# Scores' low-part product on 128 rows, and the maps' last product in 64x64 array tiles: a two-layer hybrid backbone on one Trainium2 core

## Chip, core and metric

The kernel runs on one core of a Trainium2 chip, in one launch. The metric is the device time in microseconds (us) from the first to the last instruction of an execution, with what lies around it; lower is better. TensorE multiplies (PE in the rows; PEld is its weight load), VectorE (DVE), ScalarE (ACT) and GpSimd (POOL) do the rest, and SyncE (SP) issues all DMAs in one queue, in order. Each engine works through its own instructions in the order in which they stand.

## What is computed

Two layers over 512 latent and 256 context tokens of width 1024. A layer is a gated feed-forward half, a token mixer, and a second feed-forward half. The mixer projects the tokens once and gives the columns to three groups of heads: a Fourier transform, a banded attention with six query heads on two key heads, and a recurrence in both directions. The change touches the last two. Cut to what matters here:

```python
# attention: per block of 128 queries, keys of up to three blocks and all 256 context keys
s_w = jnp.einsum('bnqhgd,bnkhd->bnhgqk', qb, kw)
s_c = jnp.einsum('bnqhgd,bchd->bnhgqc', qb, kc)
m = max(s_w.max(-1), s_c.max(-1), sink)
o = (exp(s_w - m) @ vw + exp(s_c - m) @ vc) / den

# recurrence, per head, over time, in both directions; the latent scan starts from the context's state
sa = state @ a
state = state * w + sa[..., None] * b + v[..., None] * k
y = state @ r
```

## The kernel before

**Precision.** Products that need more than one pass are made of exact splits: a float32 value is cut into a high part (float32r) and a low part, and high x high, low x high and high x low are summed in PSUM. A float32r matmul is one record in the trace. The recurrence uses plain float32 matmuls, and each of these is two records in the trace.

**Attention** (`attention`). Work goes by blocks of 128 queries: blocks 4 and 5 are context, 0 to 3 latent; the first layer does all six, the second the four latent ones. `queries(b)` loads the queries of a block for both key heads (384 KB, `q<-qd`, L1062) into the tile `t`, of which there is one buffer. ACT casts `t` to high parts in `qs` (L1064, one buffer, too), and POOL writes the low parts `t - qs` over the half of the partitions that belongs to the other key head (two instructions, L1067). So for key head v the 64 partitions of its own half hold high parts, and the other 64 hold low parts. `scores` then makes each score tile with two float32r matmuls: all 128 rows of `qs` against the keys' high parts, which lie on both halves (L1083: high x high and low x high in one), and the 64 high rows against the keys' low parts `kl` (L1084). A block has six heads; a latent head has two such pairs (256 context keys, and 256 or 384 window keys), a context head has one. That is 108 pairs: 84 of 256 columns and 24 of 384.

**Recurrence** (`rwkv`). Time is cut into chunks of 64 tokens and groups of four chunks; six groups per layer. For each group `stage_a` forms products of the operands (PSUM tiles `pa`), `inverses` inverts triangles on DVE, `stage_c` builds every chunk's map of state and values (PSUM tiles `pb`), and `chain` carries the state through the four chunks (`pz`). The last product of `stage_c` (L1350) multiplies, for each of three head pairs and four chunks, a 64-row half of AA (stationary, 128 columns) with BL (128 columns wide, or 64 in the two context groups of the second layer), one PSUM tile `ps[h]` per half. DVE adds the tiles to the maps MG (L1352), and the chain reads those. All matmuls of the recurrence go through the helper `mm`, so they have line L1261 in the trace; the last product is `pb<-HB` with stationary `64*128`.

**What sets the order.** The code is emitted group by group; every microsecond of estimated recurrence work `mm` calls `pump`, which emits steps of attention, of the next modulations (`wmod`, L251 to L272) and of the attention heads' part of the output projection (`out_part`, L1532). A scheduler then simulates the engines and places each instruction on its engine in the order of the simulated times, so a change of a wait or of an instruction's size moves others.

**Names.** `kf[0]`, `kf[1]`: the keys' high parts (`k` in rows); `kf[2]`: low parts (`kl`). `AA` and `BL` lie in the tile `HB`. `at`: PSUM tiles of attention (two). `wq`, `hh`, `pq`: other parts of the layer.

Of the kernel before, what the change touches and what calls it, by code (L numbers as in the profile page):

```python
# [32 lines left out]
# tiles of the feed-forward columns in the chunks after the first; buffers of gated products: raw (then low), high  # L33
# [5 lines left out]
class Halves:  # L39
    """Products of weights and tokens by Strassen's scheme (Winograd's form): the halves are of the  # L40
    inner dimension, of the tokens, and gates with values; 7 products of quarters instead of 8."""

    def __init__(self, net, n0, n):
        self.net, self.nc, self.w = net, net.nc, n // 2
        hi, lo = net.hT["h"], net.hT["o"]
        m = self.w
        q = lambda x, t, k: x[:, 4 * k:4 * k + 4, n0 + t * m:n0 + t * m + m]
        self.a = {f"a{t + 1}{k + 1}": (q(hi, t, k), q(lo, t, k)) for t in range(2) for k in range(2)}
        # the quarter a21 isn't needed by itself
        self.a["s3"] = self.a["a21"]  # L50

    def sums(self, anchor):
        """The second half of the work comes behind the anchor."""
# [31 lines left out]
    def weights(self, wi, c0):  # L85
        """The quarters of a tile of gates and one of values, and their sums."""
# [13 lines left out]
    def unit(self, ws, sg, pool):  # L100
        """silu(gates) * values."""
# [42 lines left out]
# buffers of the ring of weights that stay through the mixers' projections, and more: raw, split  # L144
# [3 lines left out]
class Net:  # L148
# [78 lines left out]
    def behind(self, inst, anchor=None):  # L227
        """The engine of both issues inst after the anchor."""
# [10 lines left out]
    def mod_steps(self, l, m, wp, pf):  # L239
        """Steps for the modulation m of layer l: the sums by quarters of the array, then their sums with the bias."""  # L240
# [35 lines left out]
    def mod(self, l, ms, stg, rows):  # L276
        """The modulations ms (at most two) of layer l."""
# [34 lines left out]
    def norm_cols(self, l, n, m_shift, m_scale):  # L312
        """Columns of g*(1+scale) and of shift, by stream."""
# [8 lines left out]
    def gate_row(self, l, n, m, s, half):  # L322
        """The row half*m*g, on all partitions."""
# [11 lines left out]
    # The arena's tiles hold rows in turn (4), loaded rows (2), halves of transposes (2) and gate rows (2);  # L335
    # in the feed-forward halves the sums of quarters of the normed tokens
# [18 lines left out]
    # In the passage from one part to the next the engines keep to the order of the program  # L355
# [10 lines left out]
    def squares(self, x, junk):  # L366
        """The root of the mean of the squares."""
# [18 lines left out]
    def prenorm(self, t, x, cols, xn, junk):  # L386
        """Normalises the token tile t; every second one is transposed with the one before it. Two steps."""
# [11 lines left out]
    def flush(self, rest=True):  # L399
        """Emits the transposes that were put off, behind products that needn't wait for them."""  # L400
# [8 lines left out]
    def some(self, n=1):  # L409
        """What follows the transposes, by quarters."""  # L410
        for _ in range(min(n, len(self.bits))):
            self.bits.pop(0)()
# [37 lines left out]
    def residual(self, t, o, grow, xn, po):  # L450
        """x + norm(o)*grow for the token tile t, with o's halves as they come. Three steps."""
# [3 lines left out]
        for i in range(2):  # L455
            cs = slice(i * 512, i * 512 + 512)
            # of the halves' mean squares
# [11 lines left out]
    def passage(self, toks, outs, post):  # L469
        """The last products of the tokens, by halves (outs), and what follows them, a token behind."""  # L470
# [27 lines left out]
    def load_w(self, srcs, shape):  # L498
        """Loads weights (pieces by columns, or by rows of two dimensions)."""
# [11 lines left out]
    def turning(self, j, name, shape, dt):  # L511
        """The next tile of the ring, raw (0) or split (1)."""
# [9 lines left out]
    def cut(self, x, e=None):  # L522
        """Splits x, of at most 512 columns in all, exactly: (high, low), each of float32r."""
# [9 lines left out]
    def split_w(self, srcs, shape, e=(None, None)):  # L533
        """Weights, split exactly, by halves of their first free dimension."""
# [4 lines left out]
    def prod(self, ps, w, s, c0, n):  # L539
        """Sums in ps the products of the weights w with n tokens of stream s, from c0."""  # L540
# [13 lines left out]
    def ffn(self, l, wi, wo, toks, post, last, mods=(), early=None):  # L554
        """last: loads that follow the last chunk's products with the tokens."""
# [10 lines left out]
        # the last 64 columns come first: gates and values in one tile  # L566
# [12 lines left out]
        def split_g(sg, w):  # L579
            gh = fp.tile([128, NT], F32R, name="gh", bufs=GB)  # L580
            if w == 64:
                # the low parts below the high ones
# [10 lines left out]
        def gated(sg, cs, w, pg, pu):  # L593
            """silu(gates) * values; of a tile with both, on its upper half."""
# [9 lines left out]
        def first(ch):  # L604
            """The first chunk, by pairs of token tiles, as they become ready."""
# [81 lines left out]
    def early_keys(self, l, raw):  # L687
        """The context's keys of the recurrence, while the latent tokens are on their way."""
# [10 lines left out]
    def mixer(self, l, need_ctx):  # L699
# [5 lines left out]
        with self.pool("mixo", bufs=1) as mo, ExitStack() as outer:  # L705
# [8 lines left out]
            # partial output projections: of the Fourier heads, and of the attention heads as well  # L714
            self.part = [[self.dp.tile([128, D], F32, name=f"part{l}_{j}_{i}") for i in range(6)] for j in range(2)]
            # decays over the chunks
            pcs = mo.tile([128, 2, 3, 12], F32, name="pcs")
            self.rw = dict(pcs=pcs)
            # in DRAM: head sums times values; values in token-major; queries; by direction the recurrence's
            # unit keys by the decay so far, rates and keys by its inverse, receptances by the decay  # L720
# [6 lines left out]
            # keys' high parts, on both halves, by head; low parts  # L727
# [1048 lines left out]
```

## Time and profile before

| | us |
|---|---|
| median of 3 runs | 3582.73 |
| lowest and highest run | 3574.76, 3584.79 |
| span of the profiled execution, first to last instruction | 3573.4 |
| PE busy in that span | 3262.0 (91%) |
| stretch of the recurrence and attention, first layer | 886 to 1336 |
| the same, second layer | 2756 to 3140 |

The profiled execution's own time is not listed apart from its span; the lowest of the three runs lies 1.4 us above that span and the median 9.3 us. In rows of the timeline the first number is the start in us, the second the length of a run of equal instructions with the modelled end of the last; the difference of two starts is therefore the better price. `128*128 128x256` is the stationary operand's rows and columns, then the moving operand's rows and columns.

### The profile page before, as it was taken

The page shows a single profiled execution, that of the slowest core. Times are in us where ns is not written, and L with a number is a line of the kernel's source. Part 1 is how long each engine was busy: PE and PEld are TensorE (multiplying, and loading weights), DVE is VectorE, ACT ScalarE, POOL GpSimd, SP SyncE. Part 2 cuts the span into 40 slices and gives each one's busy share as a digit, 9 for nine tenths or more (in the row PEclk, how much of TensorE's full clock was granted, in tenths as well). Part 3 has the DMA queues.
Part 4 walks back from the last instruction along what each step waited for, and adds up shares of the span by engine and source line. Part 5 has one row for each costly group of instructions (what it writes and reads, how often), then busy time and mean ns, then how long its engine had stood idle before and what let it go on. Part 6 is the DMA issues. An engine that isn't in the chain of part 4 may idle for free. (4 is left out here: it accounts for less than half of the span.)

```text
span 3573.4 us, 51830 instructions
## 1 busy us (share of the span) xinstructions
PE 3262.0 (91%) x19801; PEld 2729.5 (76%) x19801; DVE 2352.3 (66%) x4374; ACT 1378.0 (39%) x2818; POOL 809.4 (23%) x609
## 2 busy tenths in 40 slices
PE   7999998998778897999998999998995898979998
PEld 5689997776556655899997899997774676758997
DVE  4577777456466656677777767777464666467897
ACT  3333335342334334433335433335342433344444
POOL 0222222023101013322222322222041000024333
PEclk9999999999889988999999999999997878779999
DMA  5432224245667556222224222224355563253333
GB/s 179 148 119 71 71 69 138 87 141 134 153 172 177 160 187 214 60 69 68 71 71 140 61 71 65 71 71 138 97 166 119 157 157 71 68 182 89 101 107 101
DMA packets 540346, 410.13 MB, mean 115 GB/s; under 512 B 210405, under 2 KB 462188, under 8 KB 540098
## 3 DMA queue, kind: packets, MB, share of 16 engines
q1 hardware_dynamic: 540098, 406.82, 39.4%
q8 instruction: 156, 2.56, 0.3%
q14 instruction: 92, 0.75, 0.1%
HBM read 345.60 MB, written 61.16 MB: 114 GB/s over the span
## 5 line engine op out<-in xcount | busy, mean ns | idle before, releaser
L666 PE MATMUL po<-wq,gh 128*128 128x512 f32 (+1 forms) x1936 | 692.4, 408 | 43.6 <-ACT po L458 23.8
L529 ACT CAST wq<-raw 128x512 fp32r<-128x512 f32 (+1 forms) x626 | 383.7, 619 | 619.0 <-PE pq L112 438.8
L112 PE MATMUL pq<-hh,wq 128*128 128x384 f32 (+1 forms) x2432 | 612.8, 324 | 5.1 <-DVE st L132 2.1
L530 DVE TENSOR_TENSOR wq<-raw,wq 128x512 fp32r<-128x512 f32 x616 | 510.5, 838 | 102.3 <-ACT wq L529 97.0
L112 PE MATMUL pq<-arena,wq 128*128 128x384 f32 (+1 forms) x2736 | 491.5, 324 | 1.7 <-ACT st L116 1.1
L666 PEld LDWEIGHTS po<-wq,gh 128*128 128x128 f32 (+1 forms) x1936 | 368.6, 191 | 152.6 <-ACT po L458 31.0
L112 PEld LDWEIGHTS pq<-arena,wq 128*128 128x128 f32 x2736 | 451.3, 189 | 24.1 <-issue 4.3
L112 PEld LDWEIGHTS pq<-hh,wq 128*128 128x128 f32 x2432 | 431.6, 188 | 19.5 <-issue 5.7
L112 PE MATMUL pq<-ho,wq 128*128 128x384 f32 (+1 forms) x1216 | 394.1, 324 | 0.0
L666 PE MATMUL po<-wq,go 128*128 128x512 f32 x924 | 371.0, 402 | 2.6 <-DVE go L590 2.6
L529 ACT CAST wq<-t 128x512 fp32r<-128x512 f32 x228 | 140.7, 621 | 340.6 <-PE pq L112 303.2
L93 POOL TENSOR_TENSOR t<-raw 128x512 f32<-128x512 f32 x76 | 103.6, 1363 | 735.8 <-DVE wq L530 358.6
L672 DVE TENSOR_TENSOR accl<-accl,po 128x512 f32<-128x512 f32 x288 | 196.8, 684 | 100.8 <-PE po L666 99.0
L112 PEld LDWEIGHTS pq<-ho,wq 128*128 128x128 f32 x1216 | 229.3, 189 | 7.1 <-issue 0.9
L544 PE MATMUL pil<-hh,wq 128*128 128x512 f32 (+1 forms) x704 | 217.0, 387 | 7.9 <-DVE hh L432 5.6
L666 PEld LDWEIGHTS po<-wq,go 128*128 128x128 f32 x924 | 177.1, 192 | 32.5 <-DVE go L590 5.7
L530 DVE TENSOR_TENSOR wq<-t,wq 128x512 fp32r<-128x512 f32 x228 | 176.4, 779 | 28.3 <-ACT wq L529 23.5
L544 PE MATMUL pc<-hh,wq 128*128 128x256 f32 x976 | 179.1, 284 | 6.4 <-DVE hh L432 5.1
L97 POOL TENSOR_TENSOR t<-raw,t 128x512 f32<-128x512 f32 x76 | 117.1, 1540 | 283.2 <-DVE wq L530 283.1
L987 DVE TENSOR_TENSOR W<-W 96x126 f32<-96x126 f32 (+22 forms) x372 | 101.8, 275 | 113.1 <-DMA W<-d 106.1
L544 PEld LDWEIGHTS pil<-hh,wq 128*128 128x128 f32 x704 | 133.1, 200 | 39.1 <-DVE hh L432 6.0
L544 PEld LDWEIGHTS pc<-hh,wq 128*128 128x128 f32 x976 | 152.6, 191 | 7.6 <-DVE hh L432 5.9
(386 smaller groups left out, 5670.6 us busy)
## 6 DMA issues: line engine op xcount, KB each, us to landing
raw<-in_ffn_wi_dram SPq DMA_DIRECT2D x168, 512.0 KB
wmod<-in_mod_w_dram SPq DMA_DIRECT2D x52, 1024.0 KB
raw<-in_ffn_wo_dram SPq DMA_DIRECT2D x84, 512.0 KB
raw<-in_mix_w_in_dram SPq DMA_DIRECT2D x38, 512.0 KB
raw<-in_mod_w_dram SPq DMA_DIRECT2D x24, 512.0 KB
x_l<-arena SPq DMA_DIRECT2D x20, 512.0 KB
arena<-x_l SPq DMA_DIRECT2D x20, 512.0 KB
W<-opd SPq DMA_DIRECT2D x24, 384.0 KB
```

The source lines that it names most:

```text
L93: e.tensor_sub(t1, b12, b11)
L97: e.tensor_sub(t4, b21, t2)
L112: net.last_mm = nc.tensor.matmul(ps[:, :m], lhsT=w[x][:, k], rhs=a[y][:, k], start=(j == 0), stop=(j == 11))
L529: nc.scalar.copy(q[:, 0], x)
L530: (e or nc.vector).tensor_sub(q[:, 1], x, r32(q[:, 0]))
L544: inst = self.nc.tensor.matmul(ps[:, :n], lhsT=w[kt // 4][wp][:, kt % 4], rhs=self.hT[s, hp][:, kt, c0:c0 + n], start=(j == 0), stop=(j == ...
L666: mm = nc.tensor.matmul(ps, lhsT=x[r, t0:t0 + 128], rhs=w[hf][y][r], start=(j == 0), stop=(j == len(todo) - 1))
L672: self.pin(nc.vector.tensor_add(acc[t][:, cs], acc[t][:, cs], ps))
L987: e.tensor_mul(tv, LB[:, i, ro][:, :, None].to_broadcast([96, n, w]), XB[:, i, co][:, None, :].to_broadcast([96, n, w]))
```

## The change

In `queries`, POOL also fills the loaded tile `t` anew (as `z`, float32r): zeros on the half where the low parts came from, and a copy of the high parts on the other half; that is two MEMSETs and two CASTs per block. `scores` uses all 128 rows of `z` against all 128 rows of `kl`, where the key head that isn't meant meets zeros. In `stage_c` each matmul of the last product becomes two, one for each half of the output's partitions.

```diff
                 nc.gpsimd.tensor_sub(q[rr, v::2], t[rr, v::2], r32(q[rr, v::2]))
-            held["q"] = q
+            z = t.bitcast(F32R)
+            for v in range(2):
+                rr, hh = slice(64 - v * 64, 128 - v * 64), slice(v * 64, v * 64 + 64)
+                nc.gpsimd.memset(t[rr, v::2], 0.0)
+                nc.gpsimd.tensor_copy(z[hh, v::2], r32(q[hh, v::2]))
+            held["q"] = q, z
...
-            r = slice(kv * 64, kv * 64 + 64)
             h = kv * 3 + i
-            q = held["q"][:, 2 * i + kv]
+            q, z = (x[:, 2 * i + kv] for x in held["q"])

             def prod(ps, cs):
                 nc.tensor.matmul(ps, lhsT=q, rhs=kf[kv][:, cs], start=True, stop=False)
-                nc.tensor.matmul(ps, lhsT=q[r], rhs=kf[2][r, cs], start=False, stop=True)
+                nc.tensor.matmul(ps, lhsT=z, rhs=kf[2][:, cs], start=False, stop=True)
...
                     for c in range(4):
                         for h, rr in halves:
-                            mm(ps[h][:, c, :W], AA[rr, p, c], BL[rr, p, c, :W])
+                            for _, ro in halves:
+                                mm(ps[h][ro, c, :W], AA[rr, p, c, ro], BL[rr, p, c, :W])
```

Lines of the changed kernel from there on are five or six higher (L1083 becomes L1088, L1084 L1089, L1261 L1266).

TensorE in the first layer, where the first context block's scores meet the first group's last product (`pb_8156`, `pb_8157` and `pb_8194` are its PSUM tiles `ps[h]`; `at_7599` is a score tile). Before:

```order
L1261 MATMUL pb_8137<-HB_7421,QB_6636 128x128
L1261 MATMUL pb_8156<-HB_7421 128x128 x4
L1083 MATMUL at_7599<-k0_5308,qs_7567 128x256
L1084 MATMUL at_7599<-kl_5310,qs_7567 128x256
L1261 MATMUL pa_7806<-KI_6634,AtB_6632 128x128 x4
L1261 MATMUL pb_8157<-HB_7421 128x128 x4
```

and after:

```order
L1088 MATMUL at_7590<-k1_5309,qs_7567 128x256
L1266 MATMUL pb_8145<-HB_7421,QB_6636 128x128
L1266 MATMUL pb_8164<-HB_7421 64x128 x8
L1089 MATMUL at_7577<-kl_5310,q_7565 128x256
L1089 MATMUL at_7590<-kl_5310,q_7565 128x256
L1266 MATMUL pa_7810<-KI_6634,AtB_6632 128x128 x4
L1266 MATMUL pb_8165<-HB_7421 64x128 x8
```

Four matmuls of a PSUM tile became eight with half of the output's partitions each, still one tile `ps[h]` after the other, so the two tiles that alternate share their 64 rows; and at the start of a block the second matmuls of two pairs, which now read `q` (`z`), stand apart from the first ones.

TensorE in the first layer, from the last matmul of block 2's scores to block 3's first (`qs_9131` and `qs_9683` before, `qs_9186` and `qs_9751` after). Before:

```order
L1084 MATMUL at_9631<-kl_5310,qs_9131 128x384
L1261 MATMUL pz_11318<-Z_7427,MG2_7426 64x64
L1261 MATMUL pb_11292<-HB_7421 128x128 x4
L1261 MATMUL pb_11293<-HB_7421 128x128 x4
L1261 MATMUL pb_11304<-HB_7421 128x128 x4
L1261 MATMUL pb_11305<-HB_7421 128x128 x4
L271 MATMUL pf_9500<-sel4_97,macc_9497 128x2 x4
L1083 MATMUL at_9689<-k0_5308,qs_9683 128x256
```

and after:

```order
L1089 MATMUL at_9699<-kl_5310,q_9184 128x384
L1266 MATMUL pz_11513<-MG2_7426,Z_7427 64x64 x16
L1266 MATMUL pb_11547<-HB_7422,HB_7421 128x256 x2
L1266 MATMUL pz_11531<-MG2_7426,Z_7427 64x64 x8
L1088 MATMUL at_9761<-k0_5308,qs_9751 128x256
L1088 MATMUL at_9765<-k0_5308,qs_9751 128x256
L1538 MATMUL pf_9920<-ow00_9895,omh_9915 128x512
L1089 MATMUL at_9761<-kl_5310,q_9749 128x256
```

Block 3's first matmuls moved behind other work, and its second ones (L1089) further still.

SyncE at the load of block 3's queries in the first layer. Before:

```order
L251 DMA wmod_8996<-in_mod_w_dram 128x4x512 [waits DMAHW6_49,DMAHW1_49,PE_49]
L263 DMA macc_8943<-in_mod_b_dram 1x512 [waits DMAHW7_49,Activation_49]
L1062 DMA q_9681<-qd0_5304 128x6x128 [waits DMAHW3_49,Activation_49,Pool_49]
L251 DMA wmod_9081<-in_mod_w_dram 128x4x512 [waits DMAHW4_49,DMAHW0_49,PE_49]
L251 DMA wmod_9118<-in_mod_w_dram 128x4x512 [waits DMAHW1_49,PE_49]
```

and after:

```order
L1526 DMA ostg_9899<-in_mix_w_out_dram 64x512 [waits DMAHW7_49]
L1525 DMA ostg_9906<-in_mix_w_out_dram 64x512 [waits DMAHW0_49]
L1062 DMA q_9749<-qd0_5304 128x6x128 [waits DMAHW1_49,PE_49,Pool_49]
L1526 DMA ostg_9906<-in_mix_w_out_dram 64x512 [waits DMAHW2_49]
L1508 DMA om_9913<-mixd0_5288 128x3x128 [waits DMAHW3_49]
```

The load waits for PE now, since the score matmuls of the block before read the tile that it fills, and it stands some forty rows later in the queue, among the loads of the output projection.

## Rows read from the trace of the kernel before

**Rows 1.** The page: busy us, share of the span, instructions by engine.
```profile
PE 3262.0 (91%) x19801; PEld 2729.5 (76%) x19801; DVE 2352.3 (66%) x4374; ACT 1378.0 (39%) x2818; POOL 809.4 (23%) x609
```
**Rows 2.** Busy time in stretches: length, PE, PEld, DVE, ACT, POOL, granted clock, DMA.
```profile
886.00:1336.00 450.00, 370.90 (x3256) 264.86 (x3255) 259.88 (x799) 181.03 (x463) 41.94 (x42) 0.88 0.64 170
2756.00:3140.00 384.00, 343.97 (x2676) 255.94 (x2677) 224.68 (x714) 138.24 (x356) 31.93 (x32) 0.79 0.44 113
```
**Rows 3.** Waits of PE, 886 to 1336: us in total, times, longest.
```profile
PE pz L1261 <- DVE MG L1352: 22.5, 2, 13.7
```
**Rows 4.** PE timeline, scores in the first layer (start, us, line, operands, count).
```profile
1241.64 0.38 PE L1083 MATMUL at<-k,qs 128*128 128x256 f32 x1
1241.95 0.38 PE L1084 MATMUL at<-kl,qs 64*128 64x256 f32 x1
1242.26 0.44 PE L1083 MATMUL at<-k,qs 128*128 128x384 f32 x1
```
**Rows 5.** PE timeline, projection of the context, float32r of the same size.
```profile
815.16 0.28 PE L544 MATMUL pic<-hh,wq 128*128 128x256 f32 x1
815.28 0.28 PE L544 MATMUL pic<-ho,wq 128*128 128x256 f32 x1
```
**Rows 6.** Busy PE in two stretches, with the granted clock behind the count.
```profile
1239.00:1252.00 13.00, 13.00 (x141) 1.00 0.45 163
1290.00:1296.00 6.00, 5.97 (x14) 0.65 0.47 151
```
**Rows 7.** PE timeline near the lower clock level: scores, then 512 columns each.
```profile
1293.44 0.58 PE L1084 MATMUL at<-kl,qs 64*128 64x256 f32 x1
1293.95 0.58 PE L1083 MATMUL at<-k,qs 128*128 128x256 f32 x1
...
1299.14 0.63 PE L1532 MATMUL pf<-ow,om 128*128 128x512 f32 x1
1299.57 1.05 PE L1532 MATMUL pf<-ow,omh 128*128 128x512 f32 x2
```
**Rows 8.** PE timeline: the last product of one PSUM tile, moving 128 columns.
```profile
1218.14 1.16 PE L1261 MATMUL pb<-HB 64*128 64x128 f32 x8
```
**Rows 9.** PE timeline: 64x64 tiles that share neither rows nor columns.
```profile
937.97 1.09 PE L1261 MATMUL pa<-HB,KI 64*64 64x128 f32 x16
938.99 1.16 PE L1261 MATMUL pb<-HB 64*128 64x128 f32 x8
```
**Rows 10.** PE timeline: two 64-column tiles in turn on the same 128 rows.
```profile
1305.67 1.09 PE L1135 MATMUL at<-ptb,vt 128*64 128x128 f32 x14
1306.69 0.50 PE L1532 MATMUL pf<-ow,omh 128*128 128x512 f32 x1
```
**Rows 11.** PE timeline, second layer: moving 64 columns, 64x64 tiles and the last product.
```profile
2807.38 1.15 PE L1261 MATMUL pa<-W 64*64 64x64 f32 x32
2808.45 1.10 PE L1261 MATMUL pb<-HB,QB 128*128 128x64 f32 x8
2809.49 1.10 PE L1261 MATMUL pb<-HB 64*128 64x64 f32 x8
```
**Rows 12.** SyncE timeline: loads of queries, and a store of 192 KB with its reload.
```profile
906.38 0.56 SPq L1062 DMA_DIRECT2D q<-qd  x1
972.04 0.52 SPq L1062 DMA_DIRECT2D q<-qd  x1
...
2995.91 0.37 SPq L975 DMA_DIRECT2D d<-W  x1
2998.64 0.70 SPq L976 DMA_DIRECT2D W<-d  x1
```
**Rows 13.** ACT timeline: casts of the queries; in brackets the idle time before.
```profile
921.19 0.83 ACT L1064 CAST qs<-q 128x768 fp32r<-128x768 f32 x1 [10.52 <-DMA q<-qd]
1009.67 0.83 ACT L1064 CAST qs<-q 128x768 fp32r<-128x768 f32 x1 [1.02 <-PE at L1084]
```
**Rows 14.** POOL, the low parts of the queries: ns minimum, median, maximum.
```profile
L1067 POOL TENSOR_TENSOR qs<-q,qs x20: 987/994/1090, 922.2 to 3040.6; 64x384 fp32r<-64x384 f32 x20
```

## Prediction

> **What bounds the kernel now.** I read the page's busy times first: PE is busy 91% of the span, so it is the engine to look at [rows 1]. Both edits lie in the two stretches where recurrence and attention run together, 450 us in the first layer and 384 in the second. There PE is busy 370.9 and 344.0 us, 86% of the two, DVE 58%, POOL 9% [rows 2]. The rest of PE's time goes into waits for the recurrence's own chain, the longest total being the chain's matmuls that wait for DVE's sum of the maps [rows 3]. So PE time taken away here is mostly time of the kernel, though not all: where the DVE chain comes last, it only lengthens a wait.
>
> **Score pairs.** In the timeline a score's first matmul takes 0.31 us to the start of the second, and the second 0.31 us to the next [rows 4]. A float32r matmul of the same 128x256 shape in a run of equal ones takes 0.12 us [rows 5]. The second matmul of a pair has 64 rows, the first 128, so the array's tiling changes at each start, and a change costs about 0.19 us. Those rows lie at the full level of the clock, 2.4 GHz [rows 6]. Nearer the lower level, 1.2 GHz, a step of the pair takes 0.51 us [rows 7], where 512 columns without a change take 0.43 [rows 7], half of which, 0.21, is the price of 256; a change costs 0.30 there. The granted clock is 0.88 and 0.79 of full in the two stretches [rows 2], that is, at the lower level a quarter and two fifths of the time, a third in all: 0.67 x 0.19 + 0.33 x 0.30 = 0.23 us a change.
>
> I counted in the order of both kernels where two neighbours on PE differ in tiling (rows by columns of the stationary operand, rounded up to 32, 64 or 128): 977 such places before, 791 after. Of the places beside a score matmul 283 become 159, so 124 go: 124 x 0.23 = **28 us** less PE. The other 62 come from the scheduler's new order, between other kinds; they are worth between nothing and 14 us (62 x 0.23); I take the middle, **7 us**. The matmuls themselves cost the same on 64 rows as on 128: the steps of 0.31 in [rows 4] are equal for both.
>
> **The last product.** 60 PSUM tiles with moving 128 columns and 12 with 64 (of the second layer's context groups). Now a tile takes 8 records in 1.16 us [rows 8]. Afterwards it takes 16 records on 64x64 tiles, two in turn on the same 64 rows. The trace has no such pair. The nearest rows: 16 records whose tiles share neither rows nor columns take 1.09 us [rows 9]; 14 records on two 64-column tiles that share all their 128 rows take 1.09, so 16 would take 1.25 [rows 10]. From 0.07 less to 0.09 more for each of the 60: between -4 and +5 us, and I take 0, since the pair shares rows like the one and has the other's size. With moving 64 columns 32 records on 64x64 tiles take 1.15 us, so 16 take 0.6, where the last product takes 1.10 [rows 11]: 0.5 x 12 = 6 us less, of which I count **4**, as tiles that share rows were the slower kind above. So this edit is almost neutral: its matmuls are twice as many and half as wide.
>
> **How much of it is on the path.** 28 + 7 + 4 = 39 us of PE time. Of the stretches 86% is PE time [rows 2], and in the first half of the first layer the DVE chain often comes last. I take three quarters: **-29 us**; a third to all of it gives -13 to -39.
>
> **What the change adds.** The tile `t` has one buffer, and the low-part matmuls now read it until the block's last score. Before, the load of the next block's queries was issued long ahead: at 972.04, for a cast at 1009.67 that waits for PE alone [rows 12, 13]. Afterwards it waits for PE's last score of the block and then the block's first score must wait for the issue (0.56 us), the landing, ACT's cast (0.83) and one of POOL's differences (0.99) [rows 12 to 14]. The landing is 2.4 us for a smaller transfer in a quiet queue (from the store's end at 2996.28 to the reload that waits for it) and 14.2 us for the one load of queries that was waited for (from the issue's end at 906.94 to the cast) [rows 12, 13]. So the gap between two blocks is 4.8 to 16.6 us. There are eight such gaps, five in the first layer and three in the second. By the new order PE has work in them: 8 to 14 us in six of them, but only about 3 us before the last block of the first layer and 2 before that of the second (priced at about 1.1 us per 8 records of 128 columns and per 32 of 64, [rows 8, 11]). Uncovered are 2 + 3 = 5 us with quiet landings and some 66 us with landings of 14.2. I take landings of 5 us, gaps of 7.4, which gives 4.4 + 5.4, and 1 us for the second matmuls, which wait for POOL's zeros and copies as well: **+11 us**. Queued behind the waiting load on SP are loads of the output projection and of operands, behind the cast on ACT the exponentials and copies out of PSUM, behind the differences on POOL the masks and the states' start; if the landing is late, all three queues stand.
>
> POOL gets 40 instructions of half-partition size, at most 1.0 us each by the row of the difference [rows 14], 40 us in 834, on an engine that is busy 74 us there [rows 2]: no cost but for the delay counted above; at worst some of them lie ahead of an instruction of the chain, inside the bounds below. POOL's differences last 987 to 1090 ns, with a median of 994 [rows 14], beside a DVE that is busy more than half of the time, so neither seems to hold up the other much. The Trainium skill (SBUF — State Buffer, SBUF: two separate sides) says that VectorE and GpSimd share a port pair that one of them takes for a whole instruction while the other waits; by that rule the 40 added instructions could cost DVE as much as they last, which the narrow spread of POOL's own times does not bear out.
>
> **Sum.** -29 + 11 = -18 us. The profiled span is 3573.4, and the median is 9.3 us above it, as the table says; the sum is made on the span and carried to the median: 3582.7 - 18 = **3565 us**.
>
> **Rivals.**
> *No change that can be measured (0.24).* Of the PE time only a third becomes time of the kernel, because the recurrence's chain through DVE [rows 3] comes last more often than the busy share says: -13 + 11, 3581 us. For it: PE idles 119 us in the two stretches although its queue is full of filler. Against it: after the first half of the first layer PE is busy nearly all the time.
> *The loads of queries decide, slower (0.15).* Each of eight gaps costs 6 us on average, because ACT's and POOL's queues stand with PE: 48 - 29 = +19, 3602 us. It decides from 29/8 = 3.6 us a gap. For it: the one load that ACT waited for took 14.2 us behind others [rows 12, 13], and the scheduler can't know of such crowding. Against it: most gaps hold 8 us of PE work or more.
> *The new pairs don't overlap, slower (0.08).* If two column tiles on the same 64 rows run one after the other, each record costs what it costs now: 16 x 0.145 = 2.3 us instead of 1.16, +1.16 x 60 = 70 us of PE, with the 35 us saved elsewhere +35, three quarters of which is +26, and +11: 3620 us. Against it: column tiles on shared rows do run together in [rows 10], 14 records in 1.09 us against 8 in 1.16. The Trainium skill (TensorE: Matmul & The Clock Gate, Part 3: Packing small matmuls — row/col tiling) states that a weight load overlaps running matmuls only where the row group differs, which speaks for this rival; by that rule the time is the 3620 just given, and the trace disagrees for pairs of 128 rows.
> *All four tiles overlap (0.05).* 16 records at the 0.6 us of [rows 11]: -0.56 x 60 = -34 and -6; with -35 for the rest, all of it on the path, and +5: -70, 3513 us.
> That the second score matmul's 0.31 us is no change of tiling but a wait of accumulation would leave -11 of PE; it counts in the first rival. Against it: the first matmul of a pair takes just as long behind one that sums elsewhere.
>
> **How the numbers follow.** The forecast has 0.48. About a measurement's 0.3% (11 us) divides faster, same and slower: the forecast lies at -18, and a tenth of it ends within 11 us. Faster 0.43 + 0.05 = 0.48, same 0.24 + 0.05 = 0.29, slower 0.15 + 0.08 = 0.23. The range reaches from 3532, all of the PE time on the path with the cheaper bounds of the pairs, without the last rival, to 3606, which takes in the first rival and two thirds of the second.
>
> **What would show it.** Score pairs whose two starts are 0.12 to 0.14 us apart at the full level, and 0.31 only where a pair ends in another tiling; the last product's 16 records in 1.0 to 1.25 us; the cast of the queries waiting for its load at most of the eight gaps, with PE idle or held before a block's first score in two or three of them; PE busy time some 40 us lower in the two stretches, and the stretches together 15 to 25 us shorter. It is wrong if PE's waits for L1064's or POOL's tiles add up to more than 25 us, or if the 16 records take over 1.5 us.

## The result and the profile after

The changed kernel takes 3612.26 us (median of four executions, 3610.55 to 3612.9) against 3578.74 for the kernel before (median of four; the table ahead has three of them), a ratio of 1.011 with a 95% interval of 1.0085 to 1.0135. It is slower, by 34 us between the medians; the forecast was 3565 and its range ended at 3606. The profiled execution took 3612.9 us, with a span of 3611.1.

The page's line of busy times, to be held against [rows 1]:

```profile
PE 3238.8 (90%) x20377; PEld 2712.2 (75%) x20377; DVE 2356.9 (65%) x4374; ACT 1379.4 (38%) x2820; POOL 822.0 (23%) x649
```

PE works 23 us less than before and the span is 38 us longer. So PE has less to do, and waits grew by more. The groups of PE instructions of the two edits (busy us, mean ns of one, idle time ahead of them and what ended it):

```profile
L1266 PE MATMUL pb<-HB 64*64 64x128 f32 x960 | 71.5, 293 | 1.4 <-DVE HB L1350 0.6 <-DVE HB L1358 0.5 <-DVE MG L1358 0.2
L1088 PE MATMUL at<-k,qs 128*128 128x256 f32 x84 | 34.0, 414 | 35.0 <-POOL qs L1067 31.2 <-ACT pr L1111 2.9 <-ACT ob L1143 0.9
L1089 PE MATMUL at<-kl,q 128*128 128x256 f32 x84 | 26.1, 321 | 1.0 <-POOL q L1072 1.0
...
L1266 PE MATMUL pb<-HB 64*64 64x64 f32 x192 | 7.7, 226 | 0.0
```

The first products of the pairs have 31.2 us of idle time ahead of them that ends with POOL's low parts of the queries (L1067). Follow that back. The line of ACT's cast, which POOL waits for, in the view of one line (us of idle time before it, times):

```profile
its engine sat idle before it (us, times) until:
  DMA q<-qd: 72.6, 9
  issue: 21.0, 1
who waited for it (us, times):
  POOL qs L1067: 210.4, 9
```

Nine of ten casts wait for the load of their queries, 72.6 us in all; before, one did [rows 13]. One such gap step by step, from block 2 to block 3 of the first layer. PE's timeline, the last score of block 2 and the first of block 3:

```profile
1285.90 0.33 PE L1089 MATMUL at<-kl,q 128*128 128x384 f32 x1
...
1301.44 0.80 PE L1088 MATMUL at<-k,qs 128*128 128x256 f32 x2 [6.57 <-POOL qs L1067]
```

SyncE's timeline, the load and what stands behind it:

```profile
1286.30 0.56 SPq L1062 DMA_DIRECT2D q<-qd  x1
1286.90 7.89 SPq L1526 DMA_DIRECT2D ostg<-in_mix_w_out_dram  x1
```

ACT's timeline, the cast:

```profile
1299.48 0.83 ACT L1064 CAST qs<-q 128x768 fp32r<-128x768 f32 x1 [11.23 <-DMA q<-qd]
```

The last score ends at 1286.23, the load is issued 0.07 us later, and the cast starts 13.2 us after the issue; POOL and the next score follow at 1301.44. That is 15.2 us without a score. Over the eight gaps, the same reading gives 14.1 to 27.9 us, 151 in all, and from issue to cast 12.0 to 19.7 us; PE is idle for 65 of the 151 us. In two gaps of the second layer the load also stands behind other issues of SyncE's queue and goes out 3.0 and 7.3 us after the last score.

Why a load takes that long shows in stretches in which it is nearly all that moves (columns as in [rows 2]; the last two are the DMA engines' busy share and GB/s). Three loads of the changed kernel:

```profile
1116.00:1124.00 8.00, 6.63 (x42) 5.56 (x42) 3.23 (x16) 1.31 (x4) 0.00 (x0) 0.50 0.15 44
1288.00:1295.00 7.00, 5.10 (x52) 3.89 (x52) 3.02 (x8) 0.25 (x1) 0.00 (x0) 0.50 0.14 41
3093.00:3099.00 6.00, 1.97 (x32) 1.79 (x32) 1.53 (x5) 1.10 (x6) 0.00 (x0) 0.54 0.14 41
```

and the first load of the kernel before:

```profile
911.00:917.00 6.00, 2.83 (x44) 2.38 (x40) 1.29 (x2) 0.00 (x0) 0.00 (x0) 0.94 0.16 44
```

The 16 DMA engines are busy for 0.14 to 0.16 of the time, as much as two of them, and move 41 to 44 GB/s. By that rate 384 KB take some 9 us, an estimate from these rows. So most of a landing is the load's own pace, with the DMA engines nearly free, and not a crowd in the queue. Its source pattern (L1062) begins with a repetition of two, as both halves of the partitions read the same rows, and goes on in rows of 512 bytes; whether that sets the pace, no run tried.

Block 3's cast stood at 1257.78 before, so its attention begins 42 us later, and it ends the layer's attention: the last first-product of a pair starts at 1350.0 instead of 1308.9. By then PE has less other work. Busy time in that tail (length, PE, PEld, DVE, ACT, POOL, granted clock, DMA):

```profile
1290.00:1310.00 20.00, 11.30 (x58) 6.38 (x57) 6.00 (x12) 7.94 (x15) 5.66 (x8) 0.54 0.29 82
1310.00:1330.00 20.00, 16.72 (x83) 11.21 (x82) 12.91 (x38) 7.08 (x23) 3.12 (x3) 0.97 0.40 132
1330.00:1350.00 20.00, 13.97 (x67) 9.54 (x65) 6.25 (x23) 6.04 (x17) 0.00 (x0) 0.67 0.12 40
1350.00:1370.00 20.00, 12.81 (x46) 7.22 (x46) 6.05 (x14) 5.40 (x12) 0.00 (x0) 0.67 0.48 164
```

and in the kernel before, 40 us earlier:

```profile
1250.00:1330.00 80.00, 72.71 (x461) 46.23 (x460) 40.52 (x103) 31.54 (x79) 7.76 (x9) 0.87 0.53 168
```

PE is busy 55 of 80 us, against 73 before, and in three of the four slices its granted clock is 0.54 to 0.67 of full, so it stands at the lower of its two levels (1.2 and 2.4 GHz) for most of that time. Where the second layer's attention begins (its first cast, 2802.91 after 2759.85) the kernel is 43 us behind, and 38 at its end: the second layer adds nothing net.

### The profile page after: what moved, and what is told of

The parts are those of the page before. It is cut to its first block, busy times and chain, and to the rows that moved or that the text cites. A ratio compares the mean times of both kernels' runs of the same rounds, so it can differ in the third digit from the quotient of the medians.

```text
span 3611.1 us, 53021 instructions
## 1 busy us (share of the span) xinstructions
PE 3238.8 (90%) x20377; PEld 2712.2 (75%) x20377; DVE 2356.9 (65%) x4374; ACT 1379.4 (38%) x2820; POOL 822.0 (23%) x649
```

## Experiments

**Theories.** *Load theory*: the loss is the wait of the queries' load, which the change makes by keeping the loaded tile in use to the block's last score. Rivals: the last product costs more than its records show; the products on 128 rows or GpSimd's extra work cost the time; or the *order theory*, that the scheduler's new order does. No run leaves out any of the computation. Ratios are to the kernel before, run beside it; differences are between medians.

| run | edits | order | us against before | ratio [95%] |
|---|---|---|---|---|
| e1_maps_only | last product | scheduler's | +28 | 1.0091 [1.0072, 1.0109] |
| e2_scores_only | scores as changed | scheduler's | +31 | 1.0100 [1.0077, 1.0124] |
| e3_wait_only | the wait, old products | scheduler's | +47 | 1.0133 [1.011, 1.0156] |
| e4_own_z | scores, tile of its own, stores split | scheduler's | +7 | 1.0024 [1.0011, 1.0038] |
| e5_maps_pinned | last product | of before | -8 | 0.9984 [0.9968, 1.0001] |
| e6_order_only | none | of e1 | +24 | 1.0083 [1.0064, 1.0102] |
| e7_scores_pinned | as e4 | of before | +7 | 1.0032 [1.0011, 1.0053] |
| e8_both_pinned | as e4, and last product | of before | +12 | 1.0048 [1.0031, 1.0066] |
| e9_small_scores_pinned | scores, small tile | of before | -27 | 0.9927 [0.9904, 0.995] |
| e10_small_both_pinned | both, small tile | of before | -18 | 0.9952 [0.9934, 0.997] |
| e11_wait_pinned4 | the wait, old products | of before but SyncE | +74 | 1.0199 [1.0175, 1.0222] |
| e12_change_pinned4 | the whole change | of before but SyncE | +61 | 1.0171 [1.0147, 1.0195] |
| e13_small_scores | scores, small tile | scheduler's | -8 | 0.9971 [0.9959, 0.9984] |
| e14_small_both | both, small tile | scheduler's | -20 | 0.9936 [0.9916, 0.9956] |
| e15_order_layer1 | none | second layer of e1 | -16 | 0.9949 [0.993, 0.9969] |
| e16_stores_pinned | stores split alone | of before | +28 | 1.0077 [1.006, 1.0093] |
| e17_scores_mixed | as e9 | layers as in e15 | -21 | 0.9943 [0.9923, 0.9963] |
| e18_both_mixed | as e10 | layers as in e15 | -22 | 0.9938 [0.9919, 0.9957] |

### Each edit alone, and the wait alone

e1 is the kernel before with the change in `stage_c` alone:

```diff
-                            mm(ps[h][:, c, :W], AA[rr, p, c], BL[rr, p, c, :W])
+                            for _, ro in halves:
+                                mm(ps[h][ro, c, :W], AA[rr, p, c, ro], BL[rr, p, c, :W])
```

> The kernel before with the last product of the maps in 64x64 tiles, and its scores as they were. In the traces of before and after that product's records add up to 89.8 and 79.2 us of TensorE, in stretches where TensorE is busy nine tenths of the time. Load theory (the loss of the whole change lies in the queries' loads, which wait for the block before): 4 to 10 us faster, ratio 0.997 to 0.999, and layer 0 ends its attention where it did before (last score product near 1309 us). Rival (the twice as many matmuls of the last product hold up what is queued behind them): slower by 10 to 40 us, ratio 1.003 to 1.011.

It was 28 us slower, as the rival had it, though not yet for the rival's reason. e2 is the changed kernel with that edit undone.

> The changed kernel with the last product of the maps put back as it was. Load theory: it keeps the whole loss of the change and lacks the last product's gain, so 35 to 50 us slower than before, ratio 1.010 to 1.014, with ScalarE's cast of a block (L1064) waiting for its load for 60 to 80 us in total and the last score product of layer 0 near 1350 us. Rival (the last product holds things up): within 10 us of before, ratio 0.997 to 1.003.

It was 31 us slower, a little less than the load theory's 35 to 50; its casts wait 78.5 us for their loads. So each edit alone loses some 30 us, and both together lose 34: the two losses don't add. e3 keeps the zeroed tile and its wait, has the last product as before, and takes the second product back to 64 rows:

```diff
-                nc.tensor.matmul(ps, lhsT=z, rhs=kf[2][:, cs], start=False, stop=True)
+                nc.tensor.matmul(ps, lhsT=z[r], rhs=kf[2][r, cs], start=False, stop=True)
```

> The zeroed tile is made as in the changed kernel, in the place of the loaded queries, and is read by the second score product to the end of the block, but on 64 rows as before; the last product of the maps is as before. So the next block's load waits as in the change, GpSimd does the same extra work, and the products' tiling is that of before. Load theory: 35 to 60 us slower than before, ratio 1.010 to 1.017 (the wait of the change without what its products save). Rival (the products on 128 rows, or the other order of the work around them, cost the time): within 10 us of before, ratio 0.997 to 1.003.

47 us slower, with the old products and the scheduler's own order; e11, further on, sets the order aside. e4 gives the zeroed tile a place of its own, so that the load goes early again. For the space, the attention output's tile became two small ones, stored part by part:

```diff
-            z = t.bitcast(F32R)
+            z = ap.tile([128, 6, 128], F32R, name="qz", bufs=1)
...
-            if i == 0:
-                held["ob"] = ap.tile([128, 3, 128], F32, name="ob", bufs=OB)
-            nc.scalar.copy(held["ob"][:, i], o)
-            if i == 2:
-                self.dma(self.mixd[:, :3, b * 128:b * 128 + 128], held["ob"])
+            ob = ap.tile([128, 128], F32, name="ob", bufs=2)
+            nc.scalar.copy(ob, o)
+            self.dma(self.mixd[:, i, b * 128:b * 128 + 128], ob)
```

> The changed scores on 128 rows with the zeroed tile in a place of its own, so that the next block's load is free to go as early as before; GpSimd does the same extra work as in the change. The last product of the maps is as before. For the space the three parts of an attention output are stored one by one. Load theory: loads land before their casts, the last score product of layer 0 comes within 10 us of 1309 us, and the time is 3 to 20 us below before, ratio 0.994 to 0.999. Rival (GpSimd's extra copies and zeros, or the products on 128 rows, make the loss): still 20 to 40 us slower than before, ratio 1.006 to 1.011.

7 us slower: 24 better than e2, but not the expected gain. Something else was in it.

### The order

Two kernels with different instructions get different orders from the scheduler. To part the two causes, the next kernels carry the order of another kernel as a table, and each engine's instructions are chained in it (issue order alone, no wait); added instructions stand right behind their neighbours. The core of that function:

```diff
+    for text in ORDER.values():
+        raw = zlib.decompress(base64.b64decode(text))
+        k, prev = 0, None
+        for d in struct.unpack(f"<{len(raw) // 4}i", raw):
+            k += d
...
+                if prev is not None:
+                    tc.add_manual_dep(i, prev.name, dep, reason="order of issue")
+                prev = i
```

e5 is e1 in the order of before; e6 is the kernel before in the order of e1.

> The kernel before with the last product of the maps in 64x64 tiles, and every engine held to the order of before (the second half of each product stands right behind the first). Order theory (the loss of 28 us of this edit alone comes from the scheduler's other order, which leaves TensorE more short idle times and so more time at the clock's lower level): 0 to 10 us faster than before, ratio 0.997 to 1.000, and the granted clock from 886 to 1420 us is 0.86 to 0.89, as before (0.88). Rival (the 64x64 tiles themselves bring the clock down or cost more than their records show): 15 to 35 us slower, ratio 1.004 to 1.010, with a clock near 0.81 there, as in the run of that edit alone.

> The kernel before, with its last product as it was (128 columns stationary), but every engine held to the order which the scheduler gave the kernel that has only the last product changed. Order theory: 20 to 35 us slower than before, ratio 1.005 to 1.010, granted clock from 886 to 1420 us near 0.81. Rival (the 64x64 tiles themselves): within 8 us of before, ratio 0.998 to 1.002, clock near 0.88.

e5 lands at 0.9984 and e6 at 1.0083: the order theory's numbers in both. The same instructions in another order cost 24 us. Busy time in three stretches of the first layer, the kernel before (columns as above):

```profile
886.00:1180.00 294.00, 223.42 (x2090) 163.64 (x2090) 169.93 (x547) 115.66 (x298) 29.54 (x27) 0.87 0.69 167
1180.00:1300.00 120.00, 118.71 (x1049) 82.46 (x1046) 75.34 (x223) 54.91 (x143) 7.44 (x10) 0.93 0.53 160
1300.00:1420.00 120.00, 89.50 (x350) 62.15 (x349) 67.44 (x108) 46.91 (x103) 38.38 (x33) 0.86 0.72 227
```

and e6:

```profile
886.00:1180.00 294.00, 230.68 (x2040) 167.50 (x2038) 160.89 (x528) 116.38 (x298) 26.69 (x27) 0.83 0.66 163
1180.00:1300.00 120.00, 104.34 (x859) 75.46 (x857) 61.25 (x184) 39.56 (x101) 7.50 (x9) 0.82 0.46 133
1300.00:1420.00 120.00, 99.37 (x453) 64.64 (x452) 55.10 (x117) 34.99 (x81) 14.15 (x14) 0.77 0.56 181
```

From 1180 to 1300 the kernel before keeps PE busy nearly without a break, at a granted clock of 0.93, and gets 1049 matmul records done; e6 gets 859 done, with 14 us more idle time and a clock of 0.82. The maps are late, group by group. DVE's last sum of the last group's maps (timeline), before and e6:

```profile
1263.12 0.69 DVE L1352 TENSOR_TENSOR MG<-MG,pb 128x512 f32<-128x512 f32 x1 [0.66 <-PE pb L1261]
```

```profile
1318.16 0.69 DVE L1352 TENSOR_TENSOR MG<-MG,pb 128x512 f32<-128x512 f32 x1 [0.59 <-PE pb L1261]
```

In e6 some of the filler (attention and its outputs) stands ahead of the recurrence's work, and what waits holds up what is queued behind it. One case, PE's timeline before and e6: a group's products, in e6 behind a transpose (L1129) that waits for an exponential.

```profile
951.97 1.16 PE L1261 MATMUL pa<-KI,AtB 128*128 128x128 f32 x8
```

```profile
962.84 0.69 PE L1129 MATMUL at<-ident,pr 128*128 128x128 f32 x2 [10.86 <-ACT pr L1115]
963.32 1.91 PE L1261 MATMUL pa<-KI,AtB 128*128 128x128 f32 x8
```

How much of the loss comes from such places was not taken apart. e15 tells the layer.

> The kernel before, held to its own order up to the output projection of the first layer, and from there to the order which the scheduler gave the kernel with the last product alone changed. If that order loses in the first layer alone, as the granted clock by stretches suggests: within 8 us of before, ratio 0.996 to 1.002. If it loses in both layers alike: 10 to 18 us slower, ratio 1.003 to 1.005. If in the second layer: 25 us or more, ratio above 1.007.

With e1's order in the second layer alone the time is 16 us below before, better than any of its expectations. So, by difference, that order loses some 40 us in the first layer and wins 16 in the second: an order by itself moves this kernel by amounts as large as the edits.

### The scores without the wait

> The scores on 128 rows, with the zeroed tile in a place of its own, and every engine held to the order of before; the zeroed tile's four instructions stand right behind the differences on GpSimd; the last product is as before. This gives the price of the pairs with neither the load's wait nor another order. Load and order theory: 5 to 20 us faster than before, ratio 0.994 to 0.9985. Rival (GpSimd's extra work delays the second products, or 128 rows cost more): 5 to 20 us slower, ratio 1.0015 to 1.006.

> Both edits with the zeroed tile in a place of its own, and every engine held to the order of before. Load and order theory: 10 to 28 us faster than before, ratio 0.992 to 0.997, as both edits save TensorE time and nothing gives it back. Rival (either edit costs by itself what the whole change lost): 10 to 40 us slower, ratio 1.003 to 1.011.

Both were slower than before, by 7 and 12 us, against the load theory, although their loads go early. The trace names another wait: ACT's copies of attention outputs into the small tiles of e4, the view of that line in e7:

```profile
its engine sat idle before it (us, times) until:
  DMA mixd<-ob: 57.0, 9
```

ACT waits 57 us for stores to leave the two buffers, and PE 28.4 us for ACT. My edit for the space, in this order, had brought a wait of the very kind under study. e16 is the kernel before with those stores alone:

> The kernel before in its own order, with the attention output of a block stored in three parts from two small buffers, as in the first three runs with the zeroed tile in a place of its own. Store theory: TensorE waits 20 to 35 us for the copies of attention outputs and the time is 20 to 35 us above before, ratio 1.0055 to 1.010. Rival (the stores cost nothing, and the small zeroed tile is what gained): within 6 us, ratio 0.998 to 1.002.

28 us slower, with PE's waits for those copies (us, times, longest)

```profile
PE at L1083 <- ACT ob L1137: 25.9, 7, 7.7
```

The store theory holds for the pinned kernels, so e7 and e8 say nothing on the scores. But two buffers alone don't make the wait. e16's table puts a block's first two stores right ahead of the third, where the kernel before has its single one; ACT's copies and SyncE's stores of the first block:

```profile
943.93 0.27 ACT L1137 COPY ob<-at 128x128 f32<-128x128 f32 x1 [3.23 <-PE at L1135]
968.40 0.27 ACT L1137 COPY ob<-at 128x128 f32<-128x128 f32 x1 [0.19 <-PE at L1135]
983.92 9.76 SPq L1138 DMA_DIRECT2D mixd<-ob  x3
993.08 0.27 ACT L1137 COPY ob<-at 128x128 f32<-128x128 f32 x1 [9.47 <-DMA mixd<-ob]
```

In e4 the first two stores go out 0.3 and 0.6 us after the start of their copies, none of its copies waits for a store, and PE waits 0.4 us for them. So e4's 7 us are not this wait; its order is the scheduler's own, and what loses there is not shown. e9 and e10 keep the stores as before, and make the zeroed tile small: two pairs of heads in turn, zeros written once per layer.

```diff
+        def zeroed(copy, q, i):
+            for v in range(2):
+                hh = slice(v * 64, v * 64 + 64)
+                self.extra[copy(held["z"][hh, 2 * (i % 2) + v], r32(q[hh, 2 * i + v])).ins.name] = "after"
...
+            if "z" not in held:
+                held["z"] = z = ap.tile([128, 4, 128], F32R, name="qz", bufs=1)
...
+            q, z = held["q"][:, 2 * i + kv], held["z"][:, 2 * (i % 2) + kv]
```

> The scores on 128 rows in the order of before, the last product as before, the attention outputs stored whole again as in before. For the space the zeroed tile holds two pairs of heads in turn; its zeros are written once per layer, and a pair's high parts are copied in by GpSimd (third pair: ScalarE). Store theory (the two pinned runs with the zeroed tile in a place of its own lost their time where TensorE waited 23 to 30 us for the copy of an attention output, whose two small buffers wait for their stores): that wait is back at about 3 us, as before, and the time is 5 to 20 us below before, ratio 0.994 to 0.9986. Rival (the products on 128 rows or the copies for them cost the time): still 5 to 20 us slower than before, ratio 1.0014 to 1.006.

> As the run before, with the maps' last product in 64x64 tiles as well: both edits, in the order of before, without the load's wait. Store theory: 10 to 28 us faster than before, ratio 0.992 to 0.997. Rival: slower by up to 20 us, ratio 1.000 to 1.006.

e9 is 27 us faster than before, more than the 5 to 20 expected: the pairs on 128 rows are worth that, once nothing waits for them. e10, with the last product as well, is 18 us faster. The page's line of e9, and its groups of the pairs:

```profile
PE 3225.7 (91%) x19801; PEld 2714.3 (76%) x19801; DVE 2354.4 (66%) x4374; ACT 1381.9 (39%) x2838; POOL 823.8 (23%) x653
```

```profile
L1094 PE MATMUL at<-k,qs 128*128 128x256 f32 x84 | 33.6, 403 | 2.3 <-ACT ob L1151 2.0 <-ACT pr L1117 0.2
L1095 PE MATMUL at<-kl,qz 128*128 128x256 f32 x84 | 25.4, 306 | 0.0
```

PE is busy 36 us less than in [rows 1], and the change's 35 us of waits ahead of the pairs are down to 2.3. POOL works 14 us more, and PE waits no longer for it than before.

### The wait in a fixed order, and the change without it

> The load's wait by itself, without another order: the zeroed tile is made in the place of the loaded queries and read to the end of the block, with the second products on 64 rows and the last product as before, and TensorE, VectorE, ScalarE and GpSimd held to the order of before; SyncE's DMAs alone may move. Load theory (the wait costs by itself): 15 to 45 us slower than before, ratio 1.004 to 1.0125, with ScalarE's casts waiting 60 us or more for the loads. Order theory (the run with the wait and the scheduler's own order lost its 47 us through the order): within 10 us of before, ratio 0.997 to 1.003.

> The whole change as it is, with TensorE, VectorE, ScalarE and GpSimd held to the order of before, and SyncE's DMAs alone free to move. Load theory: the wait stays, the gains of both edits come off it, 0 to 30 us slower than before, ratio 1.000 to 1.0085. Order theory: 8 to 25 us faster than before, ratio 0.993 to 0.998.

With four engines in the order of before, the wait alone costs 74 us and the whole change 61, both more than the load theory's bounds. Against e10, the same two edits in the order of before without the wait, the whole change loses 79. The view of the cast's line in e11:

```profile
its engine sat idle before it (us, times) until:
  DMA q<-qd: 143.2, 9
```

The order of before was made for loads that come early. The scheduler's own order for the change is made with the wait in it; from e12 to the change ACT's idle time falls from 141.7 to 72.6 us and the loss from 61 to 34. e13 and e14 have no wait and the scheduler's own order.

> The scores on 128 rows with the small zeroed tile (two pairs of heads in turn, no wait of the load), the last product as before, and the scheduler's own order. Load theory (the changed scores lose by the load's wait alone, and gain 26 us where it is gone): 10 to 30 us faster than before, ratio 0.991 to 0.997. Rival (the scheduler's order for these products costs as well): within 10 us of before or slower, ratio 0.997 to 1.008.

> The same with the maps' last product in 64x64 tiles: both edits without the load's wait, in the scheduler's own order. Load theory (in the change as it is the wait is the whole loss): 5 to 25 us faster than before, ratio 0.993 to 0.9985. Rival (the last product brings the scheduler's slower order again, as it did alone): 15 to 35 us slower, ratio 1.004 to 1.010.

e14, both edits without the wait, is 20 us faster than before; its casts wait for one load, 10.2 us, as before. Its edits differ from the changed kernel's in the place and size of the zeroed tile (and the copies that fill it) alone, and it is 54 us better, with whatever the scheduler's other order adds or takes. So the wait is shown at 74 to 79 us with four engines in a fixed order, more than the whole loss, and at 38 to 54 in the scheduler's own (e13 to e2, before to e3, e14 to the change), where order is mixed in. e13 is only 8 us faster where the same products in the order of before gave 27, which again is order.

> The scores on 128 rows with the small zeroed tile, the last product as before; the first layer in the order of before, the second in the order that was 18 us faster by itself. If the two gains (26 and 18 us) add up: 30 to 45 us faster than before, ratio 0.9875 to 0.9915. If both come from the same waits of the second layer: 15 to 30 us faster, ratio 0.9915 to 0.996.

> The same with the last product in 64x64 tiles. If that product saves what its records show (10 us of TensorE): 0 to 8 us below the run beside it, its ratio 0.000 to 0.002 lower. If its smaller tiles give that back: 5 to 15 us above it, its ratio 0.0015 to 0.004 higher.

The gains of e9 and of e15's order don't add up: 21 and 22 us. Between e17 and e18 the last product makes a difference of 0.0005, too small to measure. e9, e10, e14, e17 and e18 all beat both kernels, with intervals that overlap.

## Why the prediction was wrong

**The step that failed** is the landing of the loads: "I take landings of 5 us, gaps of 7.4". From issue to cast it is 12.0 to 19.7 us, and a gap lasts 14.1 to 27.9 us. I had one measured landing of that very load, 14.2 us [rows 12, 13], and one of a smaller transfer in a quiet queue, 2.4, took the first for crowding and a value near the second. It was the load's own pace: 41 to 44 GB/s with the DMA engines 0.14 to 0.16 busy, in the kernel before as well. The far end of my own bound was 66 us for the gaps; PE is idle for 65 us in them, the wait alone measured 74 in the order of before (e11), 47 in the scheduler's (e3), and its removal 54 (from the change to e14). With 66 in place of 10 the sum would have come to 38 us above before, where 34 was measured. The Trainium skill (SBUF — State Buffer, The DMA setup-cost knee) prices a transfer at some 2 us and its bytes at 436 GB/s, which for 384 KB is an estimate of 2.9 us; the trace disagrees by a factor of four to seven, as this load moves at a tenth of that rate.

**Where it is paid** I had not seen either. I looked for PE work to fill each gap, and most gaps had some: PE's waits for POOL's low parts are only 31.2 us, and PE is busy for 86 of the 151. The rest is that attention as a whole runs late, and block 3, with its chain of small steps, ends the first layer with PE idle for 25 of 80 us and mostly at the lower clock level. The rival of the loads, at 6 us a gap and 3602, had this mechanism and too small a price; I gave it 0.15.

**Score pairs.** The price came out near, in part by luck. The forecast of 28 us of PE time is the one to hold against e9, as the other 7 were for the scheduler's order and e9 has that of before: e9 saves 36. Three quarters of 28 on the path is 21, and e9 gains 27. But the step inside a pair fell from 0.31 us to 0.22, not to 0.12. PE's timeline of the changed kernel, in a stretch with a granted clock of 0.97:

```profile
1322.31 0.38 PE L1088 MATMUL at<-k,qs 128*128 128x256 f32 x1
1322.53 0.28 PE L1089 MATMUL at<-kl,q 128*128 128x256 f32 x1
1322.74 0.39 PE L1088 MATMUL at<-k,qs 128*128 128x256 f32 x1
1322.96 0.28 PE L1089 MATMUL at<-kl,q 128*128 128x256 f32 x1
1323.08 0.39 PE L1538 MATMUL pf<-ow,omh 128*128 128x512 f32 x1
```

Only from the last L1089 to the output projection is it 0.12. So half of the 0.19 that I called a change of tiling is something else, which no run here names. And the records of the pairs add up to only 13 us less in e9 than before; where the rest of the 36 lies was not taken apart (the granted clock of the second layer's stretch, 2765 to 3106, is 0.86 in e9 and 0.81 before).

**Last product.** Right in its records, as far as it went. Sixteen of them in 1.09 us, within the 1.09 to 1.25 of [rows 9, 10]:

```profile
1263.58 1.09 PE L1266 MATMUL pb<-HB 64*64 64x128 f32 x16
```

Column tiles on the same 64 rows do run together, and the rival in which they don't, at 2.3 us for 16 records, is out. So the trace disagrees here with the rule of the Trainium skill (TensorE: Matmul & The Clock Gate, Part 3: Packing small matmuls — row/col tiling) that a weight load overlaps running matmuls only where the row group differs: the weight loads of these 16 records start with them at 1263.58 and last 0.85 us in all, within the same 1.09. In a fixed order the edit measures 8 us faster alone (e5, interval to 1.0001), 9 us slower beside the scores (from e9 to e10, intervals that overlap) and nothing in the mixed order (e17, e18): "almost neutral". What I left out is that its doubled instructions make the scheduler find another order, and that this order alone costs 24 us (e6; the edit with it 28, e1). I had counted the new order as a gain of 0 to 14 us, by tilings. In the changed kernel itself that loss shows only in part: its last maps are summed by 1281 us, against 1264 before and 1319 in e6; what ends its first layer late is the attention.

**POOL's work**: no cost that shows, as forecast. DVE's busy time differs by 5 us in 2352, and e9 gains with the extra work in it.

**The signs named ahead**: the casts do wait for their loads at every gap, the 16 records take 1.09 us, and PE's waits for POOL's tiles, 31.2 us, exceed the 25 named as the mark of being wrong. The pairs' starts 0.12 to 0.14 us apart did not come, nor did shorter stretches.

## What to carry to other kernels

A buffer that is kept in use longer turns a load made ahead into a load in the chain: price it from issue to use at the landing which the same transfer shows, look at the rate at which it moves before calling that crowding, and ask which stage it makes the last one. Where a scheduler orders the work, compare an edit in a fixed order as well; otherwise the order's own swing, here from 16 us faster to 24 us slower with not one instruction changed, is taken for the edit's effect. A space-saving edit in an experiment is an edit, too, and so is the place that a fixed order gives it: both want a run of their own.

## What the runs showed of the hardware

A load of 384 KB from DRAM landed 12 to 20 us after its issue at nine blocks, and moved at 41 to 44 GB/s with the DMA engines 0.14 to 0.16 busy. A wait for it is followed by a lower granted clock of TensorE (0.54 from 1290 to 1310 us, where PE was busy 11.3 of 20 us). Two PSUM-output halves of 64 columns, with stationary tiles on the same 64 rows, run together: 1.09 us for 16 records against 1.16 for 8 of double width. Score matmuls of equal tiling start 0.21 to 0.22 us apart, within a pair and from pair to pair, where a run of equal projection matmuls starts every 0.12 [rows 5]; why is open.
